# First-layer mixing weights: the trailing half by VectorE from a raw load, and the first query and key tile in the scores' banks

## The chip, the cores and the metric

The kernel runs on one core of a Trainium2 chip. The metric is the device time of one execution in microseconds, lower is better. Beside the time of whole runs there is one execution that the hardware profiler recorded, and every view below is of that one.

## The reference

The reference is two layers of a bidirectional encoder on 512 tokens of 1024 features. What matters of it:

```
for l in range(2):
    h = rmsnorm(x, g_mix[l])
    q, k, v, x_rec, gate = split(h @ w_in[l])          # 512 columns each
    att = neighbourhood_attention(q, k, v, rel_bias[l])   # 8 heads of 64, softmax over 128 keys
    xc  = depthwise_conv(x_rec)                           # width 4
    rec = (rg_lru forward + rg_lru backward)(xc) * gelu(gate)
    x = x + concat(rmsnorm(att), rmsnorm(rec)) @ w_out[l]
    h = rmsnorm(x, g_ffn[l])
    u_act, u_lin = split(h @ w_up[l])
    x = x + (gelu(depthwise_conv(u_act)) * u_lin) @ w_down[l]
return rmsnorm(x, g_final)
```

All of it is float32.

## The kernel before

Activations lie transposed: features on the 128 partitions, the 512 tokens along the row. A product of float32 accuracy is made from three passes of TensorE in a shorter format (fp32r). Each factor is split in a leading half `hi`, its value rounded to fp32r, and a trailing half `lo`, the value minus `hi`, and `mm3` (L247 to L250) adds `a.hi*b.hi + a.hi*b.lo + a.lo*b.hi` into one PSUM bank. So every weight block that arrives from memory has to be turned into such a pair.

The weights lie in memory as a list of chunks in the order of their use (`weight_plan`), each 128 rows by 1024 columns (512 KB; a chunk of gate blocks has 512 columns). `chunk` hands out the next pair, and before it does so it calls `split_to` and `load_to`, which issue the work for later chunks. There are three ways to a pair:

- most chunks: SP loads `raw` by DMA, ScalarE copies it to `hi` (L210), VectorE subtracts `lo = raw - hi` (L211). `raw` has 2 buffers, `hi` and `lo` 4 each;
- the first layer's mixing chunks (`by_dma`: 16 query, key, value and gate-branch columns and 4 recurrence gates; chunks 4 to 23): a DMA from GpSimd's queue converts while it loads, and leaves `hi` (L175). ScalarE then writes `-hi` into `lo` (L200), and a second GpSimd DMA loads the weights again and adds them to it (L201), which leaves `weight - hi`;
- the second layer's mixing chunks: they are split during the first layer's MLP, written to memory as halves (`split_later`) and only loaded later (L180).

A `by_dma` chunk is split at the use of the chunk two places ahead of it, and its `hi` is loaded at most three places ahead. A `hi` buffer comes free when TensorE has finished the chunk four places earlier.

A layer's mixing part begins with the recurrence branch: four banks `xr`, chunks 0 to 3. Between its passes stand the row statistics: TensorE sums squares (`cps`, L387), VectorE scales them (L389), GpSimd takes the power (L392), TensorE spreads the result over rows (L399) and ScalarE copies it to `rb` (L401). VectorE then takes the four `xr` banks to SBUF, times `rb` (L515). After that the steps of the table `MIX` follow: `q0`, `k0`, ... are the column tiles, `a` and `b` their halves, `c` the convolution, `t` the recurrence gates with their scans, `S` the scores and softmax of a head, `T` the transposes of its probabilities, `u` the turned values, `P` the products of probabilities and values, `e` the gate branch. Heads go in pairs; "the first pair" is `S0 T0 P0` with `S1 T1 P1`, and so on to the fourth.

PSUM has eight banks in four pools: `ps_mm` 3 (columns, gates), `ps_s` 2 (scores), `ps_pt` 2 (transposed probabilities), `ps_o` 1 (products). A new tile of a pool waits until the pool's oldest one has been read.

Each engine works through its own instructions in order, and waits at the first whose inputs aren't there. That order, and the order of the DMA issues in SP's and GpSimd's queues, is made by the tile framework's scheduler from the program's order and its `urgent` marks; an instruction marked so is moved ahead of others that are ready.

Of the kernel before, what the change touches and what calls it, by code (L numbers as in the profile page):

```python
# [9 lines left out]
F32 = mybir.dt.float32  # L10
F32R = mybir.dt.float32r
AF = mybir.ActivationFunctionType
ALU = mybir.AluOpType

P = 128
# [85 lines left out]
def encoder(ctx: ExitStack, tc: tile.TileContext, x_d, w_d, cols_d, bias_d, out_d):  # L101
    nc = tc.nc
    plan = weight_plan()

    def pool(name, bufs, space=None):
        kw = {"space": space} if space is not None else {}
        return ctx.enter_context(tc.tile_pool(name=name, bufs=bufs, **kw))
# [10 lines left out]
    p_raw = pool("p_raw", 2)  # L118
# [5 lines left out]
    ps_mm = pool("ps_mm", 3, PS)  # L124
    ps_s = pool("ps_s", 2, PS)
# [3 lines left out]
    def big(pl, tag, name, dt=F32):  # L129
        return pl.tile([P, T], dt, tag=tag, name=name)  # L130

    def psum(pl, name):
        return pl.tile([P, T], F32, tag="ps", name=name)
# [6 lines left out]
    def f32(ap):  # L140
        return ap.bitcast(F32)

    def urgent(level=2):
        return tc.high_priority(offset=level * URGENT) if level else ExitStack()


    raws, highs, lows, halves, kept = {}, {}, {}, {}, {}
# [3 lines left out]
    def pieces(i):  # L151
        return (slice(0, 1024),) if i else (slice(0, 512), slice(512, 1024))

    def width(i):
        return P * len(plan[i][2])

    def by_dma(i):

        w, _, bs = plan[i]
        return w == "gate" or w == "w_in" and bs[0][1] != 12  # L160

    def load_to(n):
        while state["load"] < min(n, len(plan)):
            i = state["load"]
            if by_dma(i):
                if i > state["use"] + 3:
                    return
                highs[i] = p_hi.tile([P, 1024], F32R, tag="hi", name=f"hi{i}")
                if i in kept:
                    lows[i] = p_lo.tile([P, 1024], F32R, tag="lo", name=f"lo{i}")  # L170
                    for n, t in enumerate((highs[i], lows[i])):
                        for h in range(width(i) // 512):
                            nc.sync.dma_start(f32(t[:, 512 * h:512 * h + 512]), kept[i][n, h])
                else:
                    nc.gpsimd.dma_start(highs[i][:, :width(i)], w_d[i][:, :width(i)])  # L175
                state["load"] += 1
                continue
            raws[i] = p_raw.tile([P, 1024], F32, tag="raw", name=f"raw{i}")
            for n, sl in enumerate(pieces(i)):
                nc.sync.dma_start(raws[i][:, sl], w_d[i][:, sl])  # L180
                if i == n == 0:
                    nc.sync.dma_start(x[0], x_d[0])
            state["load"] += 1

    def split_to(n):
        while state["split"] < min(n, len(plan)):
            i = state["split"]
            if by_dma(i) and i > state["use"] + 2:
                return
            load_to(i + 1)  # L190
            if i in kept:
                halves[i] = highs.pop(i), lows.pop(i)
                state["split"] += 1
                continue
            if i in highs:
                hi = highs.pop(i)
                lo = p_lo.tile([P, 1024], F32R, tag="lo", name=f"lo{i}")
                with urgent(1):
                    ws = slice(0, width(i))
                    nc.scalar.activation(lo[:, ws], f32(hi[:, ws]), AF.Copy, scale=-1.0)  # L200
                    nc.gpsimd.dma_start(lo[:, ws], w_d[i][:, ws], accum_op=ALU.add)  # L201
                halves[i] = (hi, lo)
                state["split"] += 1
                continue
            raw = raws.pop(i)
            hi = p_hi.tile([P, 1024], F32R, tag="hi", name=f"hi{i}")
            lo = p_lo.tile([P, 1024], F32R, tag="lo", name=f"lo{i}")
            with urgent(0):
                for sl in pieces(i):
                    nc.scalar.activation(hi[:, sl], raw[:, sl], AF.Copy)  # L210
                    nc.vector.tensor_tensor(out=lo[:, sl], in0=raw[:, sl], in1=f32(hi[:, sl]), op=ALU.subtract)  # L211
            halves[i] = (hi, lo)
            state["split"] += 1
# [22 lines left out]
    def chunk(w, l, first):  # L236
        i = state["use"]
        assert plan[i][0] == w and plan[i][1] == l and plan[i][2][0] == first, (plan[i], w, l, first)
        split_to(i + 1 + AHEAD_SPLIT)
        load_to(i + 1 + AHEAD_LOAD)  # L240
        state["use"] += 1
        return halves.pop(i)
# [26 lines left out]
    def column_parts(ps, w, l, m, rhs, step):  # L269
        c = chunk(w, l, (0, m))  # L270
        for k in range(8):
            mm3(ps, blk(c, k), rhs[k], k == 0, k == 7)
            if k % step == step - 1:
                yield
# [4 lines left out]
    for k in range(ND):  # L279
        x.append(p_x.tile([P, T], F32, tag=f"x{k}", name=f"x{k}"))  # L280
    nc.scalar.dma_start(cols[:, 0:8], cols_d[:, 0:8])
    load_to(1)
    for k in range(1, ND):
        nc.sync.dma_start(x[k], x_d[k])
# [120 lines left out]
    def by_group(ap):  # L405
        return ap.rearrange("p (r g c) -> p g r c", r=ROWS, c=8)

    def in_group(ap):
        return ap.rearrange("p g (r c) -> p g r c", r=ROWS)
# [82 lines left out]
    def layer(l, xn):  # L492
# [79 lines left out]
        qk = {}  # L572

        def query_tile(i):
            ps = psum(ps_mm, f"qps{l}{i}")
            yield from column_parts(ps, "w_in", l, i, xg, 4)
            with urgent():
                for n in range(2):
                    rows = slice(64 * n, 64 * n + 64)
                    nc.vector.tensor_tensor(out=in_group(q_pair[rows, :, n]), in0=by_group(ps)[rows],  # L580
                                            in1=by_group(rb)[rows], op=ALU.mult)

        def key_tile(i):
            ps = psum(ps_mm, f"kps{l}{i}")
            yield from column_parts(ps, "w_in", l, 4 + i, xg, 4)
            qk[4 + i] = big(p_h, "h", f"k{l}{i}")
            with urgent():
                nc.vector.scalar_tensor_tensor(out=qk[4 + i], in0=ps, scalar=0.125, in1=rb, op0=ALU.mult, op1=ALU.mult)
# [123 lines left out]
        def products(h, t1, t2):  # L712
# [22 lines left out]
            if h % 2:  # L735
# [6 lines left out]
                att_stats.add(at)  # L742

        tiles = {"q": query_tile, "k": key_tile, "v": value_tile, "g": gate_tile}
        going, probs, turned = {}, {}, {}
        ops, ocs, bias = {}, {}, {}
# [87 lines left out]
        for hf in range(2):  # L834
# [39 lines left out]
            for m in range(4, 6 if last else 8):  # L874
                ps = psum(ps_s if m % 2 else ps_pt, f"dn{l}{hf}{m}")
# [79 lines left out]
```

## Time and profile before

| | |
|---|---|
| median of 3 runs | 1227.52 us (1226.66 to 2701.48) |
| profiled execution, whole | 1226.75 us |
| its span on the core | 1224.0 us |
| TensorE matmul busy | 1198.3 us, 98% |
| TensorE weight load busy | 999.0 us, 82% (beside the matmuls) |
| VectorE busy | 736.7 us, 60% |
| ScalarE busy | 503.7 us, 41% |
| GpSimd busy | 123.7 us, 10% |
| mean granted TensorE clock | 0.995 |

The span runs from the core's first to its last recorded instruction; the rest of the whole time lies around it. An engine's busy share says how full it is, not whether it decides. The granted clock is the share of TensorE's full 2.4 GHz that the chip lets through.

### The profile page before, as it was taken

What the parts mean: (1) busy time and instruction counts of PE and PEld (TensorE: products, weight loads), DVE (VectorE), ACT (ScalarE), POOL (GpSimd) and SP (SyncE); (2) the same over time, 40 slices, a digit from 0 to 9 for tenths busy, and PEclk for the clock granted to TensorE, in tenths of its full rate; (3) what the DMA queues carried; (4) which work ended last, traced back from release to release, by engine and by line L of the source; (5) the groups of instructions that cost most, each with busy time, mean ns of one, the idle gap of its engine ahead of it and who ended that gap; (6) DMA issues with size and microseconds to landing.
All of it is one profiled execution on the core that took longest, in us unless ns stands there. A gap on an engine that the chain in (4) does not pass through costs nothing.

```text
span 1224.0 us, 14611 instructions
## 1 busy us (share of the span) xinstructions
PE 1198.3 (98%) x5566; PEld 999.0 (82%) x5566; DVE 736.7 (60%) x1217; ACT 503.7 (41%) x741; POOL 123.7 (10%) x206
## 2 busy tenths in 40 slices
PE   9888999999999999999999999999999999999997
PEld 7777788888888888888888888888888888888886
DVE  6476684877653376662736777677556255555454
ACT  5566783544332144332416667443322212323220
POOL 3222210022220022210000100100000000000000
PEclk9999999999999999999999999999999999999999
DMA  8656632366663366653245443142232332322322
GB/s 270 142 133 124 140 104 70 103 206 213 229 217 99 102 216 224 215 171 103 92 132 191 141 148 104 38 136 90 100 104 88 101 103 86 104 93 96 103 69 69
DMA packets 53942, 161.29 MB, mean 132 GB/s; under 512 B 6768, under 2 KB 9968, under 8 KB 53872
## 3 DMA queue, kind: packets, MB, share of 16 engines
q1 hardware_dynamic: 39328, 113.17, 28.3%
q0 software_dynamic: 14400, 47.20, 14.1%
q8 instruction: 43, 0.70, 0.2%
q14 instruction: 27, 0.22, 0.1%
q10 hardware_dynamic: 144, 0.00, 0.0%
HBM read 139.37 MB, written 20.97 MB: 131 GB/s over the span
## 4 chain that ended last, share of the span: by engine, by line
PE 90%; DVE 4%; issue 3%; DMA 1%; POOL 1%; ACT 1%; POOLq 0%; DVEq 0%; ACTq 0%
PE dn L248 7%; PE dn L250 7%; PE dn L249 7%; PE pa L248 7%; PE pl L248 7%; PE pa L249 7%; PE pl L249 7%; PE pl L250 7%; PE pa L250 7%; PE out L250 2%; PE out L248 2%; PE out L249 2%; DMA hi<-in_w 1%; PE up L248 1%; PE up L250 1%
## 5 line engine op out<-in xcount | busy, mean ns | idle before, releaser
L210 ACT ACTIVATE hi<-raw 128x1024 fp32r<-128x1024 f32 (+1 forms) x169 | 178.3, 1055 | 388.3 <-PE dn L249 160.5
L211 DVE TENSOR_TENSOR lo<-raw,hi 128x1024 fp32r<-128x1024 f32 (+1 forms) x169 | 205.3, 1215 | 133.5 <-ACT hi L210 132.7
L818 DVE TENSOR_TENSOR ua<-pa,g_ffn_rb 128x512 f32<-128x512 f32 x44 | 30.4, 692 | 113.7 <-PE pa L250 113.7
L826 ACT ACTIVATE uc<-uc,cols 128x512 f32<-128x512 f32 x48 | 34.8, 724 | 115.9 <-DVE uc L824 115.9
L827 DVE TENSOR_TENSOR uc<-pl,uc 128x512 f32<-128x512 f32 x44 | 30.3, 689 | 44.6 <-PE pl L250 43.8
L466 POOL TENSOR_TENSOR fin_r<-fin_ms,expo 128x2 f32<-128x2 f32 x2 | 1.4, 697 | 377.7 <-DVE fin_ms L464 377.7
L795 DVE TENSOR_TENSOR dns<-dn,g_ffn_rb 128x512 f32<-128x512 f32 x30 | 20.5, 689 | 29.4 <-PE dn L250 29.4
L233 POOL DMA_DIRECT2D kept<-lhi x36 | 19.5, 543 | 177.8 <-ACT lhi L227 174.5
L824 DVE SCALAR_TENSOR_TENSOR uc<-ua,cols,uc 128x511 f32<-128x511 f32 x48 | 36.0, 750 | 1.5
L822 DVE SCALAR_TENSOR_TENSOR uc<-ua,cols,uc 128x511 f32<-128x511 f32 x48 | 35.7, 744 | 0.1
L200 ACT ACTIVATE lo<-hi 128x1024 fp32r<-128x1024 f32 (+1 forms) x20 | 19.4, 972 | 32.7 <-DMA hi<-in_w 24.6
L228 DVE TENSOR_TENSOR llo<-lraw,lhi 128x512 fp32r<-128x512 f32 x36 | 24.7, 687 | 10.7 <-ACT lhi L227 10.7
L682 ACT ACTIVATE prob<-prob,mx 128x192 f32<-128x192 f32 (+1 forms) x64 | 27.5, 430 | 1.1 <-DVE mx L680 0.9
L248 PE MATMUL out<-atth,hi 128*128 128x512 f32 x64 | 25.7, 402 | 0.0
L249 PE MATMUL out<-attl,hi 128*128 128x512 f32 x64 | 25.2, 394 | 0.0
L201 POOL DMA_DIRECT2D lo<-in_w x20 | 17.5, 877 | 75.8 <-ACT lo L200 75.8
L250 PE MATMUL out<-atth,lo 128*128 128x512 f32 x64 | 25.2, 393 | 0.0
L616 POOL CAST edge<-vh 64x384 fp32r<-64x384 f32 x16 | 10.1, 629 | 144.3 <-ACT vh L611 143.8
L233 POOL DMA_DIRECT2D kept<-llo x36 | 19.5, 543 | 48.9 <-DVE llo L228 46.3
L821 DVE TENSOR_SCALAR uc<-ua,cols 128x512 f32<-128x512 f32 x48 | 23.4, 487 | 1.6
L667 PE MATMUL s<-k,q_pair 128*128 128x192 f32 (+1 forms) x128 | 22.0, 314 | 2.4 <-DVE mx L675 2.4
L556 DVE SCALAR_TENSOR_TENSOR ti<-ti,xc 128x512 f32<-128x512 f32 x16 | 11.0, 689 | 21.9 <-ACT ti L548 21.9
(934 smaller groups left out, 3687.2 us busy)
## 6 DMA issues: line engine op xcount, KB each, us to landing
raw<-in_w SPq DMA_DIRECT2D x167, 512.0 KB, 3.5
lraw<-in_w POOLq DMA_DIRECT2D x36, 256.0 KB, 4.2
kept<-lhi POOLq DMA_DIRECT2D x36, 256.0 KB, 2.5
kept<-llo POOLq DMA_DIRECT2D x36, 256.0 KB, 3.0
hi<-kept SPq DMA_DIRECT2D x36, 256.0 KB, 2.8
lo<-kept SPq DMA_DIRECT2D x36, 256.0 KB, 4.0
hi<-in_w POOLq DMA_DIRECT2D x16, 512.0 KB, 5.4
lo<-in_w POOLq DMA_DIRECT2D x16, 512.0 KB, 5.6
```

The source lines that it names most:

```text
L210: nc.scalar.activation(hi[:, sl], raw[:, sl], AF.Copy)
L211: nc.vector.tensor_tensor(out=lo[:, sl], in0=raw[:, sl], in1=f32(hi[:, sl]), op=ALU.subtract)
L233: nc.gpsimd.dma_start(d, f32(parts[h][n]))
L248: nc.tensor.matmul(ps, a[0], b[0], start=start, stop=False)
L249: nc.tensor.matmul(ps, a[0], b[1], start=False, stop=False)
L250: nc.tensor.matmul(ps, a[1], b[0], start=False, stop=stop)
L682: nc.scalar.activation(pr[b], pr[b], AF.Exp, bias=mx[:, b % 4:b % 4 + 1], accum_out=sm[:, b % 4:b % 4 + 1])
L818: nc.vector.tensor_tensor(out=ua, in0=pa, in1=rbf[0], op=ALU.mult)
L822: nc.vector.scalar_tensor_tensor(out=c[:, 1:], in0=ua[:, :T - 1], scalar=w[0], in1=c[:, 1:], op0=ALU.mult, op1=ALU.add)
L824: nc.vector.scalar_tensor_tensor(out=c[:, :T - 1], in0=ua[:, 1:], scalar=w[2], in1=c[:, :T - 1], op0=ALU.mult, op1=ALU.add)
L826: nc.scalar.activation(c, c, AF.Gelu_apprx_tanh, bias=col("conv_ffn_b", j, l))
L827: nc.vector.tensor_tensor(out=c, in0=pl_, in1=c, op=ALU.mult)
```

## The change

For chunks 4 to 23 the `-hi` copy on ScalarE and the adding DMA on GpSimd's queue are gone. In their place SP loads the chunk a second time as it is, into the two `raw` buffers, and VectorE subtracts. The subtraction is not marked urgent, the copy was (`urgent(1)`). Apart from that, the first query and the first key tile of either layer take their bank from the scores' pool.

```diff
@@ load_to
                 else:
-                    nc.gpsimd.dma_start(highs[i][:, :width(i)], w_d[i][:, :width(i)])
+                    ws = slice(0, width(i))
+                    nc.gpsimd.dma_start(highs[i][:, ws], w_d[i][:, ws])
+                    raws[i] = p_raw.tile([P, 1024], F32, tag="raw", name=f"raw{i}")
+                    nc.sync.dma_start(raws[i][:, ws], w_d[i][:, ws])
@@ split_to
-                with urgent(1):
-                    ws = slice(0, width(i))
-                    nc.scalar.activation(lo[:, ws], f32(hi[:, ws]), AF.Copy, scale=-1.0)
-                    nc.gpsimd.dma_start(lo[:, ws], w_d[i][:, ws], accum_op=ALU.add)
+                ws = slice(0, width(i))
+                nc.vector.tensor_tensor(out=lo[:, ws], in0=raws.pop(i)[:, ws], in1=f32(hi[:, ws]), op=ALU.subtract)
@@ query_tile
-            ps = psum(ps_mm, f"qps{l}{i}")
+            ps = psum(ps_mm if i else ps_s, f"qps{l}{i}")
@@ key_tile
-            ps = psum(ps_mm, f"kps{l}{i}")
+            ps = psum(ps_mm if i else ps_s, f"kps{l}{i}")
```

TensorE's order is the same in both programs. GpSimd's queue has 20 DMA issues fewer, so that its `hi` loads follow one another, with the statistics' power and the casts `edge` between them as before. SP's queue has 20 loads more, all ahead of the loads of the output projection's chunks; of those, before, the first two stood directly behind the first two tables `bias`. VectorE has 20 subtractions more (L202 in the changed program), ScalarE 20 copies fewer. The line numbers of the changed program are higher by one from L203 on.

Three places show what the scheduler made of it. The first is VectorE in the row statistics, from the reciprocal of the decay constants on (`sp_...`, small work for the recurrence); `cps` are the sums, `g_mix_ms` what GpSimd waits for. Before:

```order
L339 RECIPROCAL sp_q<-sp_s_378 128x16
L340 TENSOR_TENSOR sp_s<-sp_e,sp_q 128x16
L341 TENSOR_TENSOR sp_s_378<-sp_s 128x16
L342 TENSOR_SCALAR sp_q<-sp_s_378 128x16
L344 TENSOR_TENSOR sp_q<-sp_q,sp_s_378 128x16
```

and changed:

```order
L340 RECIPROCAL sp_q<-sp_s_382 128x16
L341 TENSOR_TENSOR sp_s<-sp_e,sp_q 128x16
L202 TENSOR_TENSOR lo_343<-raw_273,hi_271 128x1024
L390 TENSOR_SCALAR g_mix_ms<-cps_334 128x4
L342 TENSOR_TENSOR sp_s_382<-sp_s 128x16
```

The subtraction of chunk 5 now stands directly ahead of the statistics' scaling; that of chunk 4 stands seven rows earlier, behind the last sum of squares. Before, the scaling stood seven small instructions further down with no subtraction ahead of it.

The second is VectorE ahead of the scores of head 2 (`prob`, `s`; the second pair), from the recurrence's `w` of the forward direction on. Before:

```order
L555 SCALAR_TENSOR_TENSOR w_784<-a_799,w_784 128x512
L733 COPY att_732<-o_817 64x4x8x8 x2
L740 SCALAR_TENSOR_TENSOR attl_833<-att_732,cols,atth_832 128x512
L556 SCALAR_TENSOR_TENSOR ti_838<-ti_838,xc_1_634 128x512
L675 ISA prob_159,mx_887<-s_889,bias_885 128x128
```

and changed:

```order
L556 SCALAR_TENSOR_TENSOR w_796<-a_811,w_796 128x512
L202 TENSOR_TENSOR lo_876<-raw_794,hi_792 128x1024
L741 SCALAR_TENSOR_TENSOR attl_845<-att_742,cols,atth_844 128x512
L557 SCALAR_TENSOR_TENSOR ti_850<-ti_850,xc_1_643 128x512
L202 TENSOR_TENSOR lo_959<-raw_880,hi_878 128x1024
L676 ISA prob_159,mx_900<-s_902,bias_898 128x128
```

Two subtractions of 1024 columns (chunks 14 and 15) now stand ahead of the first score eviction. The third pair has the same two (chunks 19 and 20).

The third is ScalarE at the same pair: `a`, `w` are the recurrence's factors, L682 (L683) the softmax's exponentials, and the square root (L560, L561) is what the scans wait for. Before:

```order
L200 ACTIVATE lo_946<-hi_867 128x1024
L552 ACTIVATE w_784<-w_784,sp 128x512
L682 ACTIVATE prob_159,sm_888<-prob_159,mx_887 128x128
L682 ACTIVATE prob_159,sm_888<-prob_159,mx_887 128x192 x3
L554 ACTIVATE a_852<-a_849 128x512
L376 ACTIVATE rec_acc<-fb_533 128x512
L200 ACTIVATE lo_1017<-hi_949 128x512
L560 ACT_TABLE_LOAD
```

and changed:

```order
L377 ACTIVATE rec_acc<-fb_540 128x512
L553 ACTIVATE w_796<-w_796,sp 128x512
L555 ACTIVATE a_864<-a_861 128x512
L561 ACT_TABLE_LOAD
L561 ACTIVATE w_796<-w_796 128x1024
L683 ACT_TABLE_LOAD
L683 ACTIVATE prob_159,sm_901<-prob_159,mx_900 128x128
L683 ACTIVATE prob_159,sm_901<-prob_159,mx_900 128x192 x3
```

The copies are gone, and the exponentials of the pair's first head moved from ahead of the square root to behind it. The third pair moved likewise; the fourth had this order already.

## Rows read from the trace of the kernel before

**Rows 1.** Stretches: us, busy time of each engine (instructions), granted clock, DMA share, GB/s.

```profile
30.00:66.00 36.00, 31.67 (x144) 25.33 (x145) 19.78 (x51) 20.87 (x38) 8.50 (x12) 1.00 0.62 140
66.00:102.00 36.00, 32.39 (x160) 27.36 (x159) 21.55 (x54) 20.88 (x35) 8.39 (x14) 0.95 0.63 138
102.00:138.00 36.00, 32.71 (x158) 27.57 (x157) 25.11 (x60) 26.15 (x47) 9.75 (x15) 0.95 0.64 139
210.00:650.00 440.00, 440.00 (x1954) 364.54 (x1953) 260.59 (x348) 152.34 (x195) 61.71 (x110) 1.00 0.50 166
```

**Rows 2.** TensorE's timeline, its long waits: start, us, instruction [idle before, releaser].

```profile
30.83 0.50 PE L248 MATMUL qps<-xg_g_mix_0h,hi 128*128 128x512 f32 x1 [1.47 <-DVE xrs L515]
45.96 0.50 PE L248 MATMUL vps<-xg_g_mix_0h,hi 128*128 128x512 f32 x1 [1.01 <-ACT ti L548]
55.97 0.81 PE L667 MATMUL s<-k,q_pair 128*128 128x192 f32 x4 [2.39 <-DVE mx L675]
...
72.49 0.39 PE L248 MATMUL o<-pt,vh 128*128 128x256 f32 x1 [2.81 <-ACT vh L611]
...
110.84 0.39 PE L249 MATMUL o<-pt,vh 128*128 128x256 f32 x1 [2.87 <-ACT lo L200]
...
147.07 0.39 PE L249 MATMUL o<-pt,vh 128*128 128x256 f32 x1 [1.95 <-ACT lo L200]
```

**Rows 3.** One slice just behind the wait at 72.49 (columns as before).

```profile
75.00:76.00 1.00, 1.00 (x7) 1.00 (x6) 0.97 (x2) 0.00 (x0) 0.38 (x1) 0.50 1.07 213
```

**Rows 4.** The page's groups: the two steps that go (busy, mean ns, idle before).

```profile
L200 ACT ACTIVATE lo<-hi 128x1024 fp32r<-128x1024 f32 (+1 forms) x20 | 19.4, 972 | 32.7 <-DMA hi<-in_w 24.6
L201 POOL DMA_DIRECT2D lo<-in_w x20 | 17.5, 877 | 75.8 <-ACT lo L200 75.8
```

**Rows 5.** Timelines of SP's queue, VectorE, GpSimd and TensorE around the statistics.

```profile
15.31 5.41 SPq L180 DMA_DIRECT2D raw<-in_w  x2
19.14 1.23 DVE L211 TENSOR_TENSOR lo<-raw,hi 128x1024 fp32r<-128x1024 f32 x1 [1.33 <-ACT hi L210]
20.28 0.75 DVE L358 SCALAR_TENSOR_TENSOR xg_g_mix_7l<-x,cols,xg_g_mix_7h 128x512 fp32r<-128x512 f32 x1
24.26 0.15 DVE L389 TENSOR_SCALAR g_mix_ms<-cps 128x4 f32<-128x4 f32 x1
24.56 1.32 POOL L392 TENSOR_TENSOR g_mix_r<-g_mix_ms,expo 128x4 f32<-128x4 f32 x1
25.93 0.65 PE L399 MATMUL g_mix_rps<-ident,g_mix_r 128*128 128x128 f32 x4
```

**Rows 6.** Timelines of GpSimd and ScalarE: issues of `hi`, and the copies that awaited them.

```profile
46.17 1.40 POOL L175 DMA_DIRECT2D hi<-in_w  x2
53.06 1.06 ACT L200 ACTIVATE lo<-hi 128x1024 fp32r<-128x1024 f32 x1 [2.38 <-DMA hi<-in_w]
...
74.81 0.56 POOL L175 DMA_DIRECT2D hi<-in_w  x1
78.60 1.07 ACT L200 ACTIVATE lo<-hi 128x1024 fp32r<-128x1024 f32 x1 [0.66 <-DMA hi<-in_w]
```

**Rows 7.** The page's DMA issues: count, KB each, median us from issue to landing.

```profile
raw<-in_w SPq DMA_DIRECT2D x167, 512.0 KB, 3.5
```

**Rows 8.** Timelines of TensorE and VectorE: second pair's scores and transposes, fourth pair's.

```profile
93.95 1.36 PE L667 MATMUL s<-k,q_pair 128*128 128x192 f32 x8
101.13 0.60 PE L699 MATMUL ptw<-ident,prob 128*128 128x128 f32 x4
...
166.21 1.36 PE L667 MATMUL s<-k,q_pair 128*128 128x192 f32 x8
172.56 1.56 DVE L686 TENSOR_SCALAR prob<-prob,sm 128x128 f32<-128x128 f32 x4
```

**Rows 9.** Timelines of GpSimd and VectorE, fourth pair: the casts `edge`, one beside a subtraction.

```profile
172.87 1.13 POOL L616 CAST edge<-vh 64x384 fp32r<-64x384 f32 x2 [18.10 <-ACT vh L611]
175.94 1.93 POOL L616 CAST edge<-vl 64x384 fp32r<-64x384 f32 x2 [1.94 <-DVE vl L612]
175.72 1.22 DVE L211 TENSOR_TENSOR lo<-raw,hi 128x1024 fp32r<-128x1024 f32 x1
```

## The prediction

> **What bounds the kernel now.** I first read the page's table of busy times: TensorE is busy for 98% of the span. The stretches show where it isn't: from 210 to 650 us it is busy 440.00 us of 440.00, while between 66 and 138 us it lacks 3.61 and 3.29 us in each 36 us, at a mean granted clock of 0.95 [rows 1]. So the kernel is bound by TensorE, and the only slack that this change can reach lies in the first layer's mixing part, some 30 to 180 us. What is won or lost there is kept to the end, since TensorE has no free time behind it that could absorb it.
>
> Then I read TensorE's timeline for its waits. Six are of a microsecond or more in that part: 1.47, 1.01, 2.39, 2.81, 2.87 and 1.95 us, 12.50 together [rows 2]; beside them stand waits of 0.15 to 0.5 us, which I leave out on both sides. The clock adds to them: just behind the wait of 2.81 us, slices show a granted clock of 0.50, the lower of the two levels (1.2 GHz) [rows 3]; over 36 us a mean of 0.95 is 0.05 x 36 = 1.8 us lost. The next stretch has the same mean around the wait of 2.87 us. In the stretch 30 to 66, which has the wait of 2.39 us, it stayed at 1.00 [rows 1], so I count no loss behind that and the shorter ones. All that can be won is so 12.5 + 3.6 = 16.1 us, 1.3% of the time.
>
> Who makes TensorE wait: the last two rows name the copy `-hi`, the first three of the others VectorE or ScalarE. The groups tell why. ScalarE stood 24.6 us in front of the copies waiting for `hi` to land, and GpSimd's queue stood 75.8 us in front of the adding DMAs waiting for the copies [rows 4]. So a late `hi` stops ScalarE, whose softmax and `vh` are queued behind, and the adding DMA holds back the next `hi` in its queue.
>
> **The change, part by part.**
>
> *Copy and adding DMA removed.* 20 x 0.97 = 19.4 us leave ScalarE, and its 24.6 us of blocking with them. VectorE gets 16 subtractions with a pitch of 1.14 us (19.14 to 20.28 [rows 5]) and 4 of half the size, some 20.5 us; in the stretch 102 to 138 its 25.1 us of 36 become some 30. That fits, so what counts is where the subtractions stand. A subtraction blocks VectorE until its `hi` and its `raw` are there. `hi` landed 6.9 us after its issue beside a second `hi` and an adding DMA (46.17 to 53.06), and after 3.8 us with little beside it (74.81 to 78.60) [rows 6]. Now no adding DMA stands in GpSimd's queue, so `hi` is issued when its buffer comes free; I take landings near 3.8 to 5 us, since the raw load that replaces the adding DMA is issued earlier than that was, and keep 6.9 us as the other end.
>
> *First query tile, -1.47 us.* The tile no longer waits for the `xr` eviction. There is no other wait ahead of it: the scores' banks hold only the warm-up product by then.
>
> *Row statistics, +1.6 us, new.* Before, `g_mix_ms` started at 24.26, GpSimd's power ran from 24.56 to 25.88 and TensorE took it at 25.93 without a wait [rows 5]: no slack, each delay of `g_mix_ms` is TensorE's. Now chunk 5's subtraction stands directly ahead. Its raw load takes the buffer of chunk 3, free at 20.37, which is the second issue in the row of 15.31. Landing takes 3.5 us at the median of such loads [rows 7], at the worst the 6.9 us of the `hi` above. So the subtraction starts at 23.9 to 27.3, `g_mix_ms` at 25.0 to 28.4: 0.8 to 4.1 us late. I take 1.6, nearer the median, which is of the same kind of load.
>
> *First value tile, -1.01 us.* It waited for a bank of `ps_mm` that a gate product held. With query and key in the scores' banks, `ps_mm` has a bank for it. The scores themselves need query and key read anyway, so these banks cost nothing there. The second layer's first tiles have no wait of this kind to lose; zero.
>
> *Second scores, -1.7 us of 2.39.* They waited for VectorE's eviction of the first scores, queued behind `w`, which waited for ScalarE, blocked until 53.06 by a copy [rows 6]. Now chunk 9's subtraction stands ahead instead. At 3.8 us of landing the wait is gone, at 6.9 us it stays whole: 0 to -2.39.
>
> *First products, -3.6 us.* Wait 2.81 and clock 1.8, 4.6 together; the copy that blocked ScalarE ahead of `vh` is gone, and the work before it is earlier by what the two former points give. At the late landings the chain over VectorE (one half subtraction more) still ends only some 1.5 us earlier than before: -1.5 to -4.6. I take -3.6, as the wait goes and the clock may still fall.
>
> *Second pair, -3.5 us.* The products' wait with its clock, 2.87 + 1.8 = 4.67, goes, since `pt` was late by a blocked ScalarE. But the exponentials of the pair's first head now follow the square root, so its transposes are late next. The fourth pair has run in that order all along: its first probabilities came 172.56 - 166.21 = 6.35 us after the start of the second scores [rows 8]. In the second pair TensorE wants them 101.13 - 93.95 = 7.18 us after, a margin of 0.83. Against it stand half a subtraction (0.6) among the scans and the two subtractions ahead of the first eviction, which delay it by 0 to 2.5 us as `hi` lands after 3.8 to over 6 us; I take 1.4. New wait: 0.6 + 1.4 - 0.83 = 1.2 us (0 to 2.3; at the late end the clock may fall, 1.8 more). Net -3.5 (-4.7 to -0.6).
>
> *Third pair, -0.7 us.* The same, but the old wait was 1.95 and no clock is counted behind it: -1.95 + 1.2 (-1.95 to +2.1).
>
> *Other moves.* The output projection's first two raw loads were issued at 15.3 and 20.4 us, far ahead; now they queue behind 20 more, but their buffers come free at the subtractions of chunks 22 and 23, more than 10 us ahead of their use: nothing. In SP's queue a table `bias` waits for the evictions of the pair before, and the raw load behind it with it; that load is for a chunk some 20 us off: nothing.
>
> **Sum:** -1.47 + 1.6 - 1.01 - 1.7 - 3.6 - 3.5 - 0.7 = -10.4 us. The profiled execution took 1226.75 us, so 1216.4; it lies 0.8 below the median of the runs, which makes **1217 us**. All best ends together give -15.4 (1212), all worst ends +1.7 (1229).
>
> A rule against the change: a cast `edge` took 1.93 us where a subtraction ran beside it and 1.13 where none did [rows 9]. The Trainium skill, SBUF — State Buffer, section Who interferes with whom, says that a VectorE instruction with two SBUF inputs contends with a GpSimd instruction that reads SBUF; the rows agree. By that rule each subtraction that meets a cast adds 0.8 us to a product's wait. One of the 20 stands directly behind `vl`, where the casts run; with it the sum would be -9.6. I leave it out, since the casts meet other two-input work there already.
>
> **Rivals.**
>
> *Half given back (24%), 1223 us.* The raw loads slow `hi` as the adding DMAs did, and it lands after 6 to 7 us. For it: the same bytes are moved as before; the DMA share was 0.63 [rows 1]. Against: the short landing in a quiet stretch. Then the second scores gain nothing, the first products 1.5, the second pair 4.67 - 2.3 = 2.4, the third loses 0.35: -1.47 + 1.6 - 1.01 - 1.5 - 2.4 + 0.35 = -4.4. The Trainium skill says in DMA: Bandwidth & Descriptors, section Issuing engines are not separate DMA queues, that transfers from all queues share the same 16 DMA engines and interleave; by that rule this case is the likely one, and no row so far shows a raw load beside a `hi` in this part.
>
> *VectorE's queue becomes the wait (8%), 1239 us.* The one that ends slower: `hi` or `raw` lands after some 8 us, VectorE stands still ahead of score evictions and statistics, and TensorE behind it. Evictions that are 4.4 us later than at 3.8 us of landing make the new wait of the second and third pair 5.6 us, with the clock 7.4: +2.7 and +5.4. The statistics cost 4.1 and 1.8 of clock, the rest gains 1.47 and 1.01: +11.5 us. It decides from landings of about 6.5 us on, where the sum passes zero. Against it: no `hi` with one other transfer beside it took so long.
>
> *Nothing moves (5%), 1227 us.* TensorE's waits come back at the same places behind VectorE instead of ScalarE. Against it: the named releasers are the removed copies.
>
> The forecast has 61%; the last 2% are for a larger gain, up to the 16 us that can be won at all.
>
> **Range:** 1211 to 1227 leaves out the slower rival, half of the third and what might lie below: some 14%. About 2% (24.5 us) can be told from no change here. No case gains that much, since 16.1 is all there is; one in fifty each for what I haven't seen, on either side.
>
> **What would show it.** Right: no wait at `qps`, the `vps` and the second `s`; a wait of 1 to 2 us at `g_mix_rps`; at the second and third pair the wait moves from `o` to `ptw`, named after `prob`; clock 1.00 around 75 us. Wrong: VectorE idle before L202 for DMA `hi` by more than 10 us in all, `o` still waiting for `vl` or `edge`, or waits in the output projection.

## The result and the profile after

The changed kernel takes 1211.53 us at the median of four runs (1210.60 to 1213.39), beside 1227.09 for the kernel before; the ratio is 0.9878 with an interval of 0.9859 to 0.9897, a gain of some 15 us. The ratio leaves out the one run of the kernel before that took 2701.48 us, which the median of 1227.09 counts. A later repeat gave 1212.91 and 0.9887 (0.9873 to 0.9902). Forecast were 1217 us, in a range of 1211 to 1227; the median lies half a microsecond inside its lower end, and two of the four runs (1210.60 and 1210.77) lie below it. The profiled execution took 1212.30 us; its span of 1210.2 us is 13.8 us shorter than before.

The page's busy times, for the whole span:

```profile
PE 1195.4 (99%) x5566; PEld 998.0 (82%) x5566; DVE 756.2 (62%) x1237; ACT 485.7 (40%) x721; POOL 105.6 (9%) x186
```

The stretches of [rows 1] again (us, busy time of PE, PEld, VectorE, ScalarE, GpSimd, granted clock, DMA share, GB/s):

```profile
30.00:66.00 36.00, 35.23 (x169) 29.33 (x168) 30.51 (x70) 18.72 (x36) 6.30 (x10) 1.00 0.47 156
66.00:102.00 36.00, 35.57 (x184) 30.21 (x185) 33.78 (x72) 22.67 (x44) 5.49 (x11) 1.00 0.53 167
102.00:138.00 36.00, 34.27 (x167) 28.46 (x166) 28.93 (x64) 21.98 (x41) 4.83 (x9) 0.95 0.44 139
210.00:650.00 440.00, 440.00 (x1959) 364.88 (x1959) 256.76 (x358) 158.78 (x207) 61.82 (x110) 1.00 0.51 169
```

TensorE is short by 0.77, 0.43 and 1.73 us where it was short by 4.33, 3.61 and 3.29. VectorE is near its limit in the second stretch, 33.78 of 36. The last row is as full as before: the change reaches only the first layer's mixing part. Note the last two columns too. From 30 to 66 us more is moved per second than before (156 GB/s for 140) with a smaller share of the DMA engines (0.47 for 0.62). That turned out to be the clue.

TensorE's timeline, the places of [rows 2] and the waits that are new (start, us, instruction, idle before and releaser):

```profile
26.36 0.65 PE L400 MATMUL g_mix_rps<-ident,g_mix_r 128*128 128x128 f32 x4 [0.23 <-POOL g_mix_r L393]
29.61 0.39 PE L249 MATMUL qps<-xg_g_mix_0h,hi 128*128 128x512 f32 x1
43.21 0.39 PE L249 MATMUL vps<-xg_g_mix_0h,hi 128*128 128x512 f32 x1
49.89 1.36 PE L668 MATMUL s<-k,q_pair 128*128 128x192 f32 x8
63.29 0.28 PE L249 MATMUL o<-pt,vh 128*128 128x256 f32 x1
...
97.59 0.28 PE L249 MATMUL o<-pt,vh 128*128 128x256 f32 x1
...
116.37 1.46 PE L668 MATMUL s<-k,q_pair 128*128 128x192 f32 x8 [0.19 <-DVE mx L676]
125.20 0.46 PE L700 MATMUL ptw<-ident,prob 128*128 128x128 f32 x2 [1.39 <-DVE prob L687]
```

All six long waits are gone. One of over half a microsecond is new, the third pair's transposes at 125.20. What is left beside it in that part are waits of 0.15 to 0.47 us.

Slices of one microsecond behind that wait, and the slice of [rows 3]:

```profile
75.00:76.00 1.00, 1.00 (x9) 0.92 (x9) 0.36 (x2) 0.97 (x2) 0.00 (x0) 1.00 0.39 90
126.00:127.00 1.00, 1.00 (x6) 0.96 (x6) 0.96 (x6) 0.59 (x1) 0.00 (x0) 0.64 0.97 381
127.00:128.00 1.00, 1.00 (x3) 0.75 (x3) 1.00 (x3) 0.98 (x3) 0.18 (x1) 0.50 1.11 406
```

At 75 us the clock is now 1.00. It falls to the lower level, 0.50, behind the wait of 1.39 us instead. Mark the last columns too: at 75 us before, with an adding load (issued at 71.72) under way, the DMA engines were full (1.07) at 213 GB/s; at 127 us now they are as full (1.11) at 406.

The page's group of the new subtractions, in place of [rows 4], and its row of `hi` loads (KB each, median us from issue to landing):

```profile
L202 DVE TENSOR_TENSOR lo<-raw,hi 128x1024 fp32r<-128x1024 f32 (+1 forms) x20 | 22.6, 1128 | 8.4 <-DMA hi<-in_w 7.1
hi<-in_w POOLq DMA_DIRECT2D x16, 512.0 KB, 4.5
```

VectorE stands 7.1 us for `hi`, where ScalarE stood 24.6; the same load landed 5.4 us after its issue before.

### The profile page after: what moved, and what is told of

Read it like the earlier page. It is cut to its first block, busy times and chain, and to the rows that moved or that the text cites. A ratio compares the mean times of both kernels' runs of the same rounds, so it can differ in the third digit from the quotient of the medians.

```text
span 1210.2 us, 14604 instructions
## 1 busy us (share of the span) xinstructions
PE 1195.4 (99%) x5566; PEld 998.0 (82%) x5566; DVE 756.2 (62%) x1237; ACT 485.7 (40%) x721; POOL 105.6 (9%) x186
## 4 chain that ended last, share of the span: by engine, by line
PE 87%; DVE 6%; issue 3%; DMA 1%; POOL 1%; ACT 1%; POOLq 0%; SPq 0%; DVEq 0%
PE dn L251 7%; PE dn L249 7%; PE dn L250 7%; PE pa L249 7%; PE pl L249 7%; PE pl L251 7%; PE pa L251 7%; PE pl L250 7%; PE pa L250 7%; PE out L251 2%; PE out L249 2%; PE out L250 2%; PE up L249 1%; PE up L251 1%; PE up L250 1%
## 5 line engine op out<-in xcount | busy, mean ns | idle before, releaser
L212 DVE TENSOR_TENSOR lo<-raw,hi 128x1024 fp32r<-128x1024 f32 (+1 forms) x169 | 205.4, 1216 | 132.4 <-ACT hi L211 131.7
L683 ACT ACTIVATE prob<-prob,mx 128x192 f32<-128x192 f32 (+1 forms) x64 | 27.4, 431 | 1.4 <-DVE mx L681 1.2
L202 DVE TENSOR_TENSOR lo<-raw,hi 128x1024 fp32r<-128x1024 f32 (+1 forms) x20 | 22.6, 1128 | 8.4 <-DMA hi<-in_w 7.1
L709 ACT ACTIVATE pt<-ptw 128x512 fp32r<-128x512 f32 x16 | 9.6, 597 | 39.0 <-PE ptw L700 39.0
L228 ACT ACTIVATE lhi<-lraw 128x512 fp32r<-128x512 f32 x36 | 22.1, 617 | 1.0 <-DMA lraw<-in_w 1.0
L668 PEld LDWEIGHTS s<-k,q_pair 128*128 128x128 f32 x128 | 20.7, 190 | 1.8 <-DVE mx L676 0.6
```

What stands on the lines that cost most here:

```text
L683: nc.scalar.activation(pr[b], pr[b], AF.Exp, bias=mx[:, b % 4:b % 4 + 1], accum_out=sm[:, b % 4:b % 4 + 1])
```

## The experiments

Three theories stood at the start. **A**: ScalarE's queue, stopped by the copies, held back softmax and `vh`. **B**: the adding DMAs make `hi` land late, whichever engine then waits for it. **C**: the banks of the first query and key tile carry a part of the gain.

**The two parts of the change apart.** e1 is the changed kernel with the old banks:

```diff
-            ps = psum(ps_mm if i else ps_s, f"qps{l}{i}")
+            ps = psum(ps_mm, f"qps{l}{i}")
-            ps = psum(ps_mm if i else ps_s, f"kps{l}{i}")
+            ps = psum(ps_mm, f"kps{l}{i}")
```

> The new way to the halves alone, with the first query and key tile in the old banks. Theory A (ScalarE's queue no longer stops at the copies): 1213 to 1215 us, most of the 15 us gained, with a wait of 1 to 1.5 us at the first query tile and some 1 us at the first value tile back. Rival C (the banks start everything earlier and carry the rest): 1220 us or more. Rival B (the adding DMAs gone from the queue) says the same here as theory A.

e2 is the kernel before with the new banks alone, the same lines the other way round.

> The first query and key tile in the scores' banks, the halves by copy and adding DMA as before. Theory A and rival B: 1225 to 1226 us, 1 to 2.5 us gained; the products' waits of 2 to 3 us at all three pairs stay. Rival C: 1220 us or less.

e1 took 1212.27 us (ratio 0.9883, 0.9866 to 0.9899), e2 1226.65 (1.0007, 0.9995 to 1.0019). The weights are the change; the banks alone are worth nothing. e1 came out below the 1213 to 1215 us of theory A, and the waits that A expected back at `qps` and `vps` did not come, though the banks are the old ones. ScalarE's timeline of the kernel before:

```profile
28.93 0.63 ACT L200 ACTIVATE lo<-hi 128x512 fp32r<-128x512 f32 x1 [5.32 <-DMA hi<-in_w]
29.47 0.58 ACT L401 ACTIVATE g_mix_rb<-g_mix_rps 128x512 f32<-128x512 f32 x1
```

and of e1:

```profile
27.93 0.60 ACT L402 ACTIVATE g_mix_rb<-g_mix_rps 128x512 f32<-128x512 f32 x1 [4.78 <-PE g_mix_rps L400]
```

The copy `rb`, on which the `xr` eviction waits and with it `qps`, stood behind a copy `-hi`; without that copy it ran 1.54 us earlier, in time for TensorE. In e2 the waits at the first query and value tile are gone too, but they come back further on: one of 1.36 us at the row statistics, 3.11 instead of 2.39 at the second scores, and the products' waits stay (2.30, 2.74 and 1.94). TensorE's timeline of e2:

```profile
27.23 0.65 PE L399 MATMUL g_mix_rps<-ident,g_mix_r 128*128 128x128 f32 x4 [1.36 <-POOL g_mix_r L392]
...
55.46 0.81 PE L667 MATMUL s<-k,q_pair 128*128 128x192 f32 x4 [3.11 <-DVE mx L675]
...
110.02 0.39 PE L249 MATMUL o<-pt,vh 128*128 128x256 f32 x1 [2.74 <-ACT lo L200]
```

**ScalarE freed, the adding DMA kept.** e3 is the kernel before with the new banks, and `-hi` made by VectorE:

```diff
-                    nc.scalar.activation(lo[:, ws], f32(hi[:, ws]), AF.Copy, scale=-1.0)
+                    nc.vector.tensor_scalar(out=lo[:, ws], in0=f32(hi[:, ws]), scalar1=-1.0, scalar2=None, op0=ALU.mult)
                     nc.gpsimd.dma_start(lo[:, ws], w_d[i][:, ws], accum_op=ALU.add)
```

> Banks as changed; the adding DMA stays, but the negated copy is made by VectorE in place of ScalarE. So ScalarE is free of the copies, while GpSimd's queue still holds each next load of a leading half behind an adding DMA. Theory A: 1214 to 1218 us. Rival B: 1222 us or more, since the leading halves land as late as before and now stop VectorE.

It took 1230.23 us (1.0033, 1.0020 to 1.0046). Theory A falls as the whole cause: no copy is left in front of ScalarE, and nothing was won. The page's group and TensorE's timeline of e3:

```profile
L200 DVE TENSOR_SCALAR lo<-hi 128x1024 fp32r<-128x1024 f32 (+1 forms) x20 | 12.9, 645 | 29.1 <-DMA hi<-in_w 28.1
...
57.88 2.50 PE L667 MATMUL s<-k,q_pair 128*128 128x192 f32 x7 [4.85 <-DVE mx L675]
```

The idle time moved with the instruction: VectorE now stands 28.1 us for `hi`, and the waits of TensorE go by VectorE's evictions. Whoever takes `hi` first stands still; `hi` itself is late.

**Without any converting DMA.** e4 is the changed kernel with `hi` made by ScalarE from the raw load that is there anyway:

```diff
-                    nc.gpsimd.dma_start(highs[i][:, ws], w_d[i][:, ws])
...
+                nc.scalar.activation(hi[:, ws], raws[i][:, ws], AF.Copy)
                 nc.vector.tensor_tensor(out=lo[:, ws], in0=raws.pop(i)[:, ws], in1=f32(hi[:, ws]), op=ALU.subtract)
```

> As changed, but without the converting DMA: ScalarE copies the leading half from the raw load at the place of the subtraction (not urgent), VectorE subtracts. ScalarE has its 20 copies back, at 1.05 us, but waits for a plain load (3.5 us at the median) and not for a converting one. Theory A: 1215 to 1221 us, since copies stand in ScalarE's queue again. Rival B: 1211 to 1213 us, since half of the bytes are gone and no load queues on GpSimd.

It took 1208.68 us (0.9858, 0.9843 to 0.9872), less than either theory had said. ScalarE has its 20 copies back, and even waits 12.0 us in front of them for `raw`, yet it is the fastest kernel. A copy in ScalarE's queue is no harm when what it waits for comes in time. Its second stretch:

```profile
66.00:102.00 36.00, 36.00 (x187) 30.75 (x186) 33.73 (x72) 27.38 (x50) 2.32 (x4) 1.00 0.24 75
```

TensorE is full there, with the DMA engines less than half as busy as in the changed kernel (0.24 for 0.53); in that part no wait of TensorE is longer than 0.33 us.

**How the adding DMA makes `hi` late.** Three ways were open: its wait in GpSimd's queue keeps the next `hi` from being issued (**B1**); its bytes take a share of the DMA engines (**B2**); or something in the transfer itself. e6 gives the queue the wait without the bytes, by a copy of one column of each finished `lo` (into a small tile `seen`) where the adding DMA stood:

```diff
                 nc.vector.tensor_tensor(out=lo[:, ws], in0=raws.pop(i)[:, ws], in1=f32(hi[:, ws]), op=ALU.subtract)
+                with urgent(1):
+                    nc.gpsimd.tensor_copy(seen[:, i:i + 1], f32(lo[:, 0:1]))
```

> As changed, and GpSimd's queue holds a copy of one column of each finished `lo` at the place where the adding DMA stood: no byte more is moved, but the next `hi` is issued only when a subtraction is done. If the late issue made the kernel before slow (B1): VectorE stands more than 20 us ahead of L202 for DMA `hi`, and the time is 1218 us or more. If it was the sharing of the DMA engines (B2): VectorE stands some 8 to 12 us, and the time is 1213 us or less.

e5 gives the bytes without the wait, by SP's queue:

```diff
                 nc.vector.tensor_tensor(out=lo[:, ws], in0=raws.pop(i)[:, ws], in1=f32(hi[:, ws]), op=ALU.subtract)
+                spare = p_kept.tile([P, 1024], F32, tag=f"spare{i % 4}", name=f"spare{i}")
+                nc.sync.dma_start(spare[:, ws], f32(hi[:, ws]))
```

> As changed, and SP's queue also writes each landed `hi` of the 20 chunks out to spare memory: 9.44 MB more of transfers in the first layer's mixing part, and nothing more in GpSimd's queue. If the sharing of the DMA engines is what made `hi` late before (B2): `hi` lands late again, VectorE stands more than 15 us ahead of L202, and the time is 1218 us or more. If the late issue out of GpSimd's queue did it (B1): VectorE stands less than 12 us there, and the time is 1213 us or less.

e6 took 1214.12 us (0.9896, 0.9869 to 0.9923): B1 falls. The group of its small copy (view of all groups):

```profile
L205 POOL COPY seen<-lo 128x1 f32<-128x1 f32 x20 | 8.8, 441 | 71.2 <-DVE lo L203 63.4 <-DVE sp_y L339 5.4 <-DVE g_mix_ms L393 2.4
```

GpSimd stood 63.4 us for the subtractions, not far from the 75.8 of [rows 4], but VectorE only 9.0 us ahead of its subtractions, 2.8 of them for `hi`, where B1 wanted more than 20, and the time can't be told from the changed kernel's, since the `hi` behind still landed in 4.5 us. e5 took 1216.63 (0.9907, 0.9884 to 0.9929), between the two expectations: 8.3 us of waiting for `hi`, as B1 wanted, and 4 to 5 us more time than the changed kernel, or 2 to 4 by the ratios, whose intervals overlap. Sharing may cost something, and is far from the 15 us.

So it is the transfer itself: that it adds (**B4**), or that it stands ahead of `hi` in the same queue (**B3**). e10 is e3 without the addition; every byte, queue and place stays:

```diff
-                    nc.gpsimd.dma_start(lo[:, ws], w_d[i][:, ws], accum_op=ALU.add)
+                    nc.gpsimd.dma_start(lo[:, ws], w_d[i][:, ws])
```

> As e3, but the second GpSimd load of each of the 20 chunks overwrites `-hi` with the weights instead of being added to it, so the trailing halves hold the wrong values; bytes, queue and order stay. If it is the addition that makes the second load dear (B4): `hi` lands 4.0 to 4.7 us after its issue at the median, VectorE stands less than 15 us for DMA `hi` at L200, and the time is 1220 us or less. If any load standing ahead of `hi` in GpSimd's queue delays it (B3): VectorE stands 20 to 28 us, `hi` takes over 5 us, and the time is 1226 to 1231 us, as in e3.

e12 is e6 with a write of the finished `lo` in the place of the small copy, e13 with a load over it:

```diff
+                with urgent(1):
+                    spare = p_kept.tile([P, 1024], F32, tag=f"spare{i % 4}", name=f"spare{i}")
+                    nc.gpsimd.dma_start(spare[:, ws], f32(lo[:, ws]))   # e12
+                    nc.gpsimd.dma_start(lo[:, ws], w_d[i][:, ws])       # e13, without the spare tile
```

> As e6, but at the place of the adding DMA, GpSimd's queue writes the finished `lo` out to spare memory: a plain transfer of the same size, with the issue of the next `hi` behind it. Against e5, which moved as many bytes out of SP's queue and took 1216.6: if standing behind a transfer in its own queue delays `hi` (B3), `hi` takes over 5 us at the median and the time is 1222 us or more. If not, and it is the bytes or the addition (B4), the time is 1213 to 1218 us with `hi` at 4.0 to 4.7 us.

> As e12, but the transfer at the adding DMA's place is a plain load: it writes the weights over the finished `lo`, so the trailing halves hold the wrong values. Bytes, queue and order are those of e12 (`raw` loads, `hi` loads and a third transfer). If a plain load ahead of it doesn't hold `hi` back, and it was the kind of transfer in e3 and e12 (adding, writing): `hi` takes 4.0 to 4.8 us at the median and the time is 1211 to 1217 us. If it was the sum of bytes in that queue and on the engines: `hi` takes over 5.2 us and the time is 1220 to 1226 us.

e10 took 1212.89 us (0.9883, 0.9865 to 0.9900), 17 us less than e3 (0.9883 for 1.0033; the two ran on different chips), and what the changed kernel takes. The addition is the cause. GpSimd's and VectorE's timelines of e3, one turn of the loop:

```profile
33.43 0.88 POOL L175 DMA_DIRECT2D hi<-in_w  x1
38.83 0.69 DVE L200 TENSOR_SCALAR lo<-hi 128x1024 fp32r<-128x1024 f32 x1 [1.89 <-DMA hi<-in_w]
40.06 0.87 POOL L201 DMA_DIRECT2D lo<-in_w  x1 [5.75 <-DVE lo L200]
40.62 0.87 POOL L175 DMA_DIRECT2D hi<-in_w  x1
```

and of e10:

```profile
29.50 0.54 POOL L175 DMA_DIRECT2D hi<-in_w  x1
33.63 0.69 DVE L200 TENSOR_SCALAR lo<-hi 128x1024 fp32r<-128x1024 f32 x1 [0.61 <-DMA hi<-in_w]
34.87 0.54 POOL L201 DMA_DIRECT2D lo<-in_w  x1 [4.83 <-DVE lo L200]
35.40 0.54 POOL L175 DMA_DIRECT2D hi<-in_w  x1
```

Issue, landing, negation, second issue, next issue: a turn takes 40.62 - 33.43 = 7.19 us with the addition and 35.40 - 29.50 = 5.90 without, and what shrinks is mostly the way from the issue of `hi` to the negation, 5.40 against 4.13 us. The DMA issues and the queue's share of the DMA engines, of e3:

```profile
q0 software_dynamic: 14400, 47.20, 14.0%
hi<-in_w POOLq DMA_DIRECT2D x16, 512.0 KB, 5.3
lo<-in_w POOLq DMA_DIRECT2D x16, 512.0 KB, 5.5
```

and of e10:

```profile
q0 software_dynamic: 14400, 47.20, 12.4%
hi<-in_w POOLq DMA_DIRECT2D x16, 512.0 KB, 4.1
lo<-in_w POOLq DMA_DIRECT2D x16, 512.0 KB, 3.9
```

The same 47.20 MB take 14.0% of 1228.2 us with the addition and 12.4% of 1210.8 without, 172 and 150 us. The Trainium skill says in DMA: Bandwidth & Descriptors, section Rules for kernel authors, that an accumulating DMA reads its destination and writes it later. That would be work which a plain load hasn't; no run here looked inside a transfer. But slices of one microsecond within the two turns show what it takes. Of e3, with an adding load and the `hi` behind it under way (columns as before):

```profile
43.00:44.00 1.00, 1.00 (x6) 0.81 (x5) 0.00 (x0) 0.97 (x3) 0.00 (x0) 1.00 1.02 205
```

and of e10, with a plain load and the `hi` behind it:

```profile
37.00:38.00 1.00, 1.00 (x6) 0.84 (x5) 0.00 (x0) 0.40 (x1) 0.00 (x0) 1.00 1.10 393
```

The DMA engines are full in both, and move half as much in e3. In e3 the rate rises only at the end of the turn, to 434 GB/s from 45 to 46 us.

e10 so met the expectation of B4. The other two came out less cleanly: e13 took 1216.45 us (0.9917, 0.9901 to 0.9934), the time of the first case with `hi` at 5.1, near the second; e12 met B3 with 1223.30 (0.9986, 0.9969 to 1.0004) and `hi` at 5.7. So a transfer ahead in the same queue counts too, for a write above all, though it shows only where three transfers a chunk are moved (e12, e13), not with two (e10). Beside e5, which wrote as many bytes from SP's queue, the page's rows of e12:

```profile
L202 DVE TENSOR_TENSOR lo<-raw,hi 128x1024 fp32r<-128x1024 f32 (+1 forms) x20 | 22.3, 1115 | 24.5 <-DMA hi<-in_w 19.8
hi<-in_w POOLq DMA_DIRECT2D x16, 512.0 KB, 5.7
```

and of e5:

```profile
L202 DVE TENSOR_TENSOR lo<-raw,hi 128x1024 fp32r<-128x1024 f32 (+1 forms) x20 | 22.6, 1129 | 11.3 <-DMA hi<-in_w 8.3
hi<-in_w POOLq DMA_DIRECT2D x16, 512.0 KB, 4.5
```

The Trainium skill says in DMA: Bandwidth & Descriptors, section Queues, rings and completion order, that a DMA engine serves the queues in turn, a packet at a time, so that a transfer of another queue shares the engine while one of the same queue goes ahead. These two runs agree. They are not quite alike, since e12's write waits for the subtraction as well. Why a write holds `hi` back more than a load does (5.7 against 5.1) stays open, and so does how much of the addition's price is its own work and how much the place ahead of `hi`; e10, with the place kept and no `raw` loads, takes what the changed kernel takes, and e13, with the place kept and the `raw` loads, some 4 us more.

**The best version, and the banks once more.** e7 is e4 with the old banks, run beside a repeat of e4 and of the changed kernel (its diff to e4 is that of e1).

> As e4 (no converting DMA, `hi` made by ScalarE from the raw load), with the first query and key tile back in the banks of `ps_mm`. If the banks are worth something once nothing else is late: waits of 1 to 2.5 us in all come back at `qps` and `vps`, and the time is 1 to 2.5 us above e4's. If they are worth nothing: no wait there, and the time is within 0.7 us of e4's.

> e4 once more, beside the changed kernel on the same chip: 1208 to 1209.5 us, 2 to 4 us below the changed kernel; if its lead was a difference between chips, within 1 us of it.

> The changed kernel once more, for the comparison with e4 and e7: 1211 to 1213 us.

e4 took 1208.89 us (1208.52 to 1208.98), the changed kernel 1212.91 (1210.46 to 1213.74), e7 1208.78 (1208.70 to 1208.96); the ratios to the kernel before are 0.9857 (0.9843 to 0.9872), 0.9887 (0.9873 to 0.9902) and 0.9857 (0.9842 to 0.9872). So plain loads with a copy on ScalarE beat the changed kernel by 4 us on this chip and 2.9 us between the first two runs, and the banks are worth nothing there too: in e7 no wait came back at `qps` or `vps`. Theory C falls.

## Why the prediction was right, step by step

The mechanism on TensorE's side held: long waits and a lowered clock in the first layer's mixing part, kept to the end, and gone with the adding DMAs. The gain was larger than the sum, 13.8 us of span (14.45 of the profiled execution) for 10.4, since five of the six steps were put too low; that the median still fell inside the range is in part luck. Each step is read from the start or the end of a work item of TensorE in the two traces, as the change of its lead.

- *First query tile and statistics, forecast +0.1 together, measured -1.2* (30.83 to 29.61 at `qps`). The wait of 1.47 went, but the new one at `g_mix_rps` is 0.23 instead of 1.6 us. That is the first mis-sized term. The wait at `qps` was not the bank's alone, as forecast: e1 lost it with the old bank. Timelines of SP's queue, VectorE and GpSimd after, in place of [rows 5]:

```profile
18.88 0.33 SPq L178 DMA_DIRECT2D raw<-in_w  x1
23.82 1.22 DVE L202 TENSOR_TENSOR lo<-raw,hi 128x1024 fp32r<-128x1024 f32 x1 [0.93 <-DMA raw<-in_w]
24.96 0.15 DVE L390 TENSOR_SCALAR g_mix_ms<-cps 128x4 f32<-128x4 f32 x1
25.27 1.04 POOL L393 TENSOR_TENSOR g_mix_r<-g_mix_ms,expo 128x4 f32<-128x4 f32 x1 [2.21 <-DVE sp_s L342]
```

  The subtraction came at 23.82, the early end of the 23.9 to 27.3 forecast, but by two misses that cancel: its raw load was issued at 18.88 and not at 20.37, since its buffer came free earlier, and was there some 4.9 us later and not 3.5. So `g_mix_ms` was 0.7 us late. Of these, TensorE itself came 0.2 us later, the power took 1.04 us instead of 1.32, which no step had, and 0.23 was left as a wait. In the repeat of the changed kernel the same wait is 0.44 us, in e1 and e2 1.46 and 1.36: it moves with small things.

- *First value tile, forecast -1.0, measured -1.5; its cause was incomplete.* (45.96 to 43.21 at `vps`.) The new banks take the wait at `vps` away (e2), but it is gone in e1 and e7 too, with the old ones. The bank that it waited for is read by ScalarE's `ti`: before, that ran at 45.23, behind a copy `-hi` that had waited 3.58 us for `hi`, and in e1 at 40.22.

- *Second scores, forecast -1.7, measured -2.8* (56.54 to 51.00 at the gate branch behind them, a lead of 5.5). The whole 2.39 went: the subtraction ahead waited 1.38 us for `hi` (46.20) and the scores' eviction still came in time.

- *First products with the clock, forecast -3.6, measured -4.8* (81.94 to 71.57 at the end of the next gates, a lead of 10.4). The full 2.81 and the clock at 75 us were won back; left are 0.23, 0.40 and 0.47 us.

- *Second pair, forecast -3.5, measured -5.0* (119.42 to 104.00 at the same place of the next pair, a lead of 15.4). The new wait of 1.2 us at the transposes did not come: the second scores ran from 83.58 and the first probabilities from 90.55, 6.97 us later, inside the 7.18 that [rows 8] left. The two subtractions ahead cost 0.67 us of waiting, not the 1.4 that I had charged.

- *Third pair, forecast -0.7, measured +1.2* (149.34 to 135.16 at the end of its products, a lead of 14.2, of which 13.8 were left at the end). Here the step failed in sign. The wait at `o` went, -1.95, and the one forecast at the transposes came, 1.39 for 1.2. But the clock fell behind it, which I had counted only for the late end: 0.05 x 36 = 1.8 us in the stretch from 102 to 138. VectorE after, the first subtraction at that pair:

```profile
111.47 1.23 DVE L202 TENSOR_TENSOR lo<-raw,hi 128x1024 fp32r<-128x1024 f32 x1 [1.75 <-DMA hi<-in_w]
```

  `hi` was late by 1.75 us, and the probabilities came 124.62 - 116.37 = 8.25 us after the second scores. Here VectorE's queue became the wait, as the rival had it, in one pair and for 1.39 us.

The rivals: the raw loads did not slow `hi` as the adding DMAs had; it took 4.5 us at the median instead of 5.4. The forecast's 3.8 to 5 was right, but its reason was not: I had "now no adding DMA stands in GpSimd's queue, so `hi` is issued when its buffer comes free". e6 issues it late and loses little; e10 keeps a load there and loses little; only with the addition is the gain lost. Nor were its two landings, 6.9 and 3.8 us, those of a busy and a quiet stretch: behind the second issue too the DMA share was 1.07 [rows 3], with an adding load under way; this one was issued 3.1 us ahead of `hi`, the other 0.55. Equally, "a late `hi` stops ScalarE" named the victim, not the cause: e3 moved the stop to VectorE, e4 left the copies with ScalarE. The rival's premise, "the same bytes are moved as before", was true and misleading, since an added byte takes more of the DMA engines than a loaded one. The price of the slower rival, 1239 us, is too high by its own terms: its wait of 5.6 us counts the 1.4 of the forecast once more beside the 4.4, and 0.6 + 4.4 - 0.83 = 4.2 us at both pairs would make some 1236.

The rule on casts is borne out, and would have changed little. GpSimd's and VectorE's timelines after:

```profile
64.25 2.03 POOL L617 CAST edge<-vl 64x384 fp32r<-64x384 f32 x2
64.39 1.51 DVE L202 TENSOR_TENSOR lo<-raw,hi 128x1024 fp32r<-128x1024 f32 x1
```

Both are long, the casts 2.03 us for some 1.1 and the subtraction 1.51 for 1.22. The row of casts holds two: the first, begun before the subtraction, took 0.58 us and the second 1.39, where a cast takes some 0.5 elsewhere. The Trainium skill, SBUF — State Buffer, section Who interferes with whom, lets one of the two engines stand while the other runs; the rows agree, if the subtraction stood for the rest of the first cast and the second cast for the rest of the subtraction. It happened once, and its cost is inside TensorE's 0.47 us at that `edge`.

## What to carry to other kernels

The engine that stands longest in front of a transfer names what is late, not why: ask of the late transfer what stands ahead of it in its queue, and take that away alone before moving the waiting instruction. A load that adds while it lands is not a free addition; here it cost some 1.4% of the whole kernel (1230.23 us against 1212.89 for the same load without the addition), and an engine with room (VectorE, or ScalarE for the conversion) did the same work with one wait of TensorE above half a microsecond left, or none (e4). A queue that waits for 60 us in all costs next to nothing as long as what it issues afterwards still lands in time (e6).

## What was not expected of the hardware

- TensorE's clock fell to 0.50 behind a wait of 1.39 us at 125 us, and had stayed at 1.00 over the stretch with the wait of 2.39 us in the kernel before [rows 1, 2]; in e1, a wait of 0.94 us at the same place brought no fall, but the clock was at 0.50 from 68 to 70 us behind waits of 0.38, 0.62 and 0.41 us from 64 to 67 us. The length of one wait does not tell whether it falls. The scatter of the changed kernel, its repeat included, goes with the clock: its five runs with a mean clock of 0.996 or less took 1212.3 to 1213.7 us, and the three at 0.997 or 0.998 took 1210.5 to 1210.8.
- Taking an addition out of a DMA shortened other loads: with the same bytes in the same queue the plain `hi` went from 5.3 to 4.1 us, the second load from 5.5 to 3.9, and GpSimd's issue of it from 0.87 to 0.54 us.
- The converting load lands in 4.1 to 4.5 us where a plain raw load from SP's queue takes 3.5; without it (e4) the DMA share from 66 to 102 us falls from 0.53 to 0.24, while the rate falls from 167 to 75 GB/s.
